# Softmax weights scaled on ScalarE, and another order of the steps in an attention unit

## The chip, the cores and the metric

The kernel runs on one core of one Trainium2 chip. A core has five engines with queues of their own, each of which works strictly in order: TensorE (PE, with PEld for its weight loads), VectorE (DVE), ScalarE (ACT), GpSimd (POOL) and SyncE (SP), which here issues most DMAs. The metric is the device time of one launch in microseconds (us); lower is better.

## The reference

One layer of a bidirectional encoder on x of 256 tokens by 2048 features, in float32. Cut to what matters here:

```python
h = rmsnorm(x, norm1_g)
q, k, v, u = split(h @ w_in)              # 12 query heads, 4 key heads, of 128
scores = q @ k.T * HEAD_DIM**-0.5 + alibi # |t - s| <= 128, else -1e30
m = max(scores.max(-1), sink)
p = exp(scores - m)
p = p / (p.sum(-1) + exp(sink - m))       # the softmax weights
a = rmsnorm(p @ v, attn_out_g)
f = rmsnorm(fourier(u), fourier_out_g)
x = x + concat(a, f) @ w_out
x = x + conv_ffn(rmsnorm(x, norm2_g))     # 2048 -> 2 x 5504 -> 2048
y = rmsnorm(x, normf_g)
```

## The kernel before, in words

**Products in split precision.** A float32 operand of a product is split into a high part (a rounded copy, written by ScalarE) and a low part (the rest, a subtraction on VectorE that reads the high part). A product is three matmuls or fewer: high by high, high by low, low by high. Every weight tile goes through `split` (lines 180 to 189): ScalarE's copy on L185 (128x2048), VectorE's subtraction on L186, then the load of a tile three units later on SP, which needs the raw buffer that was just split.

**Units.** The front of the kernel is a list of units, one weight tile of 1 MB each: slots 4 to 7 make v, slots 8 to 23 make the 16 heads k0, q0, q1, q2, k1, q3, and so on (`QK_ORDER`), slots 24 to 39 are the output projection. After it come the up- and down-projections, which take most of the time. `unit(i, work)` gives TensorE what is listed in `before[i]` and then the unit's own product; it then gives the other engines what is listed in `beside[i]`, splits the weights of unit i+2, and gives them `behind[i]`. All of this is written out by hand (`manual_schedule`): each engine's queue holds its instructions in the order of these calls, and an engine waits at an instruction until its operands are there.

**A head's way through the units.** The loop at L782 lists, for unit i, one step of each head that is d slots behind it:

- d=1: `qk_out` copies half of the product from PSUM on ScalarE (L637, tile `tmp`) and adds on VectorE (L639, `add`); `qk_parts` splits the result into `qT` (ScalarE L234, VectorE L235) or, for a key head, `kT` (L654, L655; a key head has one more VectorE product, L641).
- d=2: `scores` on TensorE (L665); `scores_out` on VectorE (L681 to L686: mask, maximum, `neg`); `exps` on ScalarE (L695, L699), listed behind the unit.
- d=3: `weigh` on VectorE: the sum with the sink's part (L704, `sm`), its reciprocal (L705, `ex`), and two products of 128x256 that scale the softmax weights in place (L708, `sc`). Then `turn`: a VectorE transpose of 32x32 blocks into `tb` (L715), and a DMA of `tb` to DRAM on SP (L720, `turn`).
- d=4: `fetch`: four DMAs on SP that bring the moved blocks back as `td` (L726).
- d=5: `turn_out` splits the moved blocks into `pt` (ScalarE L739, VectorE L740).
- d=6: `values` on TensorE (L768) at the head of the unit; `values_out`: a square and a split on ScalarE (L492, L234 `cat`), the low part on VectorE (L235 `cat`), a running sum on GpSimd (L497).

The last head (q11) is turned on TensorE instead (`turn_last`, L750; `turn_last_out`).

**The four kinds of unit.** Heads come in fours (k, q, q, q), so a unit has one of four sets of steps, by i modulo 4. In these texts they are called A (i = 14, 18, 22), B (15, 19, 23), C (16, 20, 24, and 12 without `turn_out` and `values`) and D (17, 21, and 13 without `values`):

| kind | TensorE, at the head of the unit | VectorE and ScalarE steps before the change, in their order |
|---|---|---|
| A | none | `qk_out` q, `turn_out`, `weigh`, `turn`, `qk_parts` q, split |
| B | `values`, `scores` | `qk_out` q, `turn_out`, `qk_parts` q, `scores_out`, `values_out`, split, `exps` |
| C | `values`, `scores` | `qk_out` q, `turn_out`, `weigh`, `turn`, `qk_parts` q, `scores_out`, `values_out`, split, `exps` |
| D | `values`, `scores` | `weigh`, `turn`, `qk_out` k, `qk_parts` k, `scores_out`, `values_out`, split, `exps` |

At the head of a unit, `values` needs the `pt` of the unit before it, and `scores` the `qT` of the unit before it. "A's steps" below are the VectorE and ScalarE steps listed beside a unit A; the head of unit B on TensorE waits for them.

Of the kernel before, what the change touches and what calls it, by code (L numbers as in the profile page):

```python
# [10 lines left out]
AF = mybir.ActivationFunctionType  # L11
ALU = mybir.AluOpType
# [84 lines left out]
def block_kernel(  # L97
# [18 lines left out]
    nc = tc.nc  # L116
# [297 lines left out]
    before, beside, behind = {}, {}, {}  # L414

    def at(when, i, f, *a):
        when.setdefault(i, []).append((f, a))
# [214 lines left out]
    qk_sb, st = {}, {}  # L632
    sq_a = ph.tile([P, S], F32, tag="sq", name="sq_a")

    def qk_out(kind, h, ps):
        tmp = ph.tile([P, S], F32, tag="tmp", name=f"tmp_{kind}{h}", bufs=2)
        nc.scalar.activation(tmp, ps[:, S : 2 * S], AF.Copy)  # L637
        add = ph.tile([P, S], F32, tag="add", name=f"add_{kind}{h}", bufs=2)
        nc.vector.tensor_tensor(add, ps[:, 0:S], tmp, ALU.add)  # L639
        if kind == "k":  # L640
            nc.vector.tensor_tensor(add, add, r1b, ALU.mult)  # L641
        st["add", kind, h] = add
# [56 lines left out]
        nc.scalar.activation(ex, neg, AF.Exp, bias=vcol(V_SINK + h))  # L699
        st["sc", h] = sc, sm, ex  # L700

    def weigh(h):
        sc, sm, ex = st["sc", h]
        nc.vector.tensor_tensor(sm, sm, ex, ALU.add)  # L704
        nc.vector.reciprocal(ex, sm)  # L705
        for b in range(2):
            s = slice(b * S, (b + 1) * S)
            nc.vector.tensor_scalar(sc[:, s], sc[:, s], ex[:, b : b + 1], None, ALU.mult)  # L708

    def turn(h):  # L710

# [70 lines left out]
    for i in range(N_QK, N_OUT + 8):  # L782
        heads = {i - s: h for (kind, h), s in slot_of.items() if kind == "q"}
        new = [kh for kh, s in slot_of.items() if i - s == 1]
        if i - 9 in range(NG):
            at(before, i, fourier_channels, i - 9)
        valued = [h for d, h in heads.items() if d == (5 if h == NH - 1 else 6)]
        for h in valued:
            at(before, i, values, h, mm if i < N_OUT else dn)
        turned = {d: h for d, h in heads.items() if h < NH - 1}  # L790
        last = {d: h for d, h in heads.items() if h == NH - 1}
        if 4 in last:
            at(before, i, turn_last, last[4])
        if i == 15:
            at(before, i, total, sq_f, "f")
        if 2 in heads:
            at(before, i, scores, heads[2])
        if 4 in turned:
            at(beside, i, fetch, turned[4])

        for kind, h in new:
            if kind == "q":
                at(beside, i, lambda k=kind, h=h: qk_out(k, h, st.pop(("ps", k, h))))
        if 5 in turned:
            at(beside, i, turn_out, turned[5])
        if 4 in last:
            at(beside, i, turn_last_out, last[4])
        if 3 in heads:
            at(beside, i, weigh, heads[3])
        if 3 in turned:  # L810
            at(beside, i, turn, turned[3])
        for kind, h in new:
            if kind == "k":
                at(beside, i, lambda k=kind, h=h: qk_out(k, h, st.pop(("ps", k, h))))
            at(beside, i, qk_parts, kind, h)
        if 2 in heads:
            at(beside, i, scores_out, heads[2])
            at(behind, i, exps, heads[2])
        for h in valued:
            at(beside, i, values_out, h)  # L820
# [60 lines left out]
    for n, (c, kq) in enumerate(OUT_ORDER):  # L881
        i = N_OUT + n
# [391 lines left out]
    i = up_index[n]  # L1274
# [156 lines left out]
```

## Time and profile before

| | |
|---|---|
| time before, median of 3 runs | 910.65 us (909.89 to 910.98) |
| the profiled execution: its time | 908.96 us |
| its span, first to last instruction | 907.2 us |
| mean granted TensorE clock | 0.998 |
| TensorE busy | 893.2 us (98% of the span) |
| VectorE busy | 753.1 us (83%) |
| ScalarE busy | 545.9 us (60%) |
| GpSimd busy | 54.3 us (6%) |

A row of the timeline has the start in us, the duration in us, the engine, the line, the operation, `out<-in` with the shapes, and in brackets the idle time of the engine just before the instruction with what ended it. Rows of instructions that follow each other closely are merged ("x2"), and their duration is then that of the group. An engine starts an instruction before the last one's results are written, so the start of the next row often lies inside the duration of this one: the distance of two starts is called a step here, and the duration counts where another engine waits for the result. In a view of waits a row has the total, the number of waits and the longest, in us. In a view by windows a row has the stretch, its length, and each engine's busy us with its number of instructions; the granted clock, the DMA engines' share and GB/s stand at its end.

### The profile page before, as it was taken

What the parts mean: (1) busy time and instruction counts of PE and PEld (TensorE: products, weight loads), DVE (VectorE), ACT (ScalarE), POOL (GpSimd) and SP (SyncE); (2) the same over time, 40 slices, a digit from 0 to 9 for tenths busy, and PEclk for the clock granted to TensorE, in tenths of its full rate; (3) what the DMA queues carried; (4) which work ended last, traced back from release to release, by engine and by line L of the source; (5) the groups of instructions that cost most, each with busy time, mean ns of one, the idle gap of its engine ahead of it and who ended that gap; (6) DMA issues with size and microseconds to landing.
All of it is one profiled execution on the core that took longest, in us unless ns stands there. A gap on an engine that the chain in (4) does not pass through costs nothing.

```text
span 907.2 us, 12781 instructions
## 1 busy us (share of the span) xinstructions
PE 893.2 (98%) x5020; PEld 804.0 (89%) x5020; DVE 753.1 (83%) x905; ACT 545.9 (60%) x661; POOL 54.3 (6%) x65
## 2 busy tenths in 40 slices
PE   9999999999999999999999999999999999999996
PEld 7899888888899999999999999999999999999885
DVE  7569888777678877889887998978988789998996
ACT  7757576655565656557565566566656566656544
POOL 0001010110000000000000000000000000000004
PEclk9999999999999999999999999999999999999999
DMA  9965666655559687677988779797888987779652
GB/s 360 340 233 174 211 231 197 229 189 191 203 228 290 219 260 235 197 264 215 295 238 276 243 271 278 256 295 232 279 243 244 308 272 255 243 245 286 213 197 92
DMA packets 40827, 220.62 MB, mean 243 GB/s; under 512 B 4512, under 2 KB 10528, under 8 KB 16448
## 3 DMA queue, kind: packets, MB, share of 16 engines
q1 hardware_dynamic: 36512, 190.06, 56.7%
q0 software_dynamic: 4112, 29.49, 17.3%
q8 instruction: 39, 0.64, 0.3%
q10 hardware_dynamic: 144, 0.26, 0.1%
q14 instruction: 20, 0.16, 0.0%
HBM read 214.81 MB, written 4.98 MB: 242 GB/s over the span
## 4 chain that ended last, share of the span: by engine, by line
PE 81%; DVE 8%; DMA 3%; issue 3%; ACT 3%; POOL 1%; SPq 1%; ACTq 0%; POOLq 0%; DVEq 0%
PE ps_val L395 17%; PE ps_gate L395 17%; PE ps_gate L397 8%; PE ps_val L397 8%; PE ps_P L1148 3%; PE ps_P L1150 3%; PE ps_P L1149 3%; PE ps_N L1148 2%; PE ps_N L1150 2%; PE ps_N L1149 2%; DVE parts L186 2%; PE ps_u L289 2%; DMA td<-turn 2%; PE ps_a L380 2%; PE ps_a L378 2%
## 5 line engine op out<-in xcount | busy, mean ns | idle before, releaser
L186 DVE TENSOR_TENSOR parts<-raw,parts 128x2048 fp32r<-128x2048 f32 (+1 forms) x129 | 293.1, 2272 | 43.4 <-ACT parts L185 42.7
L185 ACT ACTIVATE parts<-raw 128x2048 fp32r<-128x2048 f32 (+1 forms) x129 | 245.1, 1901 | 41.7 <-PE ps_a L380 11.9
L395 PE MATMUL ps_val<-hU,parts 128*128 128x512 f32 x688 | 227.7, 382 | 0.0
L395 PE MATMUL ps_gate<-hU,parts 128*128 128x512 f32 x688 | 227.3, 382 | 0.0
L397 PE MATMUL ps_val<-hU,parts 128*128 128x256 f32 x688 | 187.5, 273 | 0.0
L397 PE MATMUL ps_gate<-hU,parts 128*128 128x256 f32 x688 | 186.9, 273 | 0.0
L395 PEld LDWEIGHTS ps_val<-hU,parts 128*128 128x128 f32 x688 | 130.0, 189 | 18.1
L395 PEld LDWEIGHTS ps_gate<-hU,parts 128*128 128x128 f32 x688 | 130.0, 189 | 18.1
L397 PEld LDWEIGHTS ps_val<-hU,parts 128*128 128x128 f32 x688 | 132.0, 192 | 0.8
L397 PEld LDWEIGHTS ps_gate<-hU,parts 128*128 128x128 f32 x688 | 131.8, 192 | 0.9
L926 ACT ACTIVATE ft_g<-ps_gate 128x256 f32<-128x256 f32 x43 | 16.5, 384 | 112.9 <-PE ps_gate L397 110.3
L395 PE MATMUL ps_q<-hT,parts 128*128 128x512 f32 x192 | 62.2, 383 | 0.0
L926 ACT ACTIVATE ft_v<-ps_val 128x256 f32<-128x256 f32 x43 | 16.5, 383 | 73.3 <-PE ps_val L397 73.3
L1148 PE MATMUL ps_P<-parts_P,op_P 128*128 128x512 f32 x144 | 54.7, 380 | 0.0
L1149 PE MATMUL ps_P<-parts_P,op_P 128*128 128x512 f32 x144 | 54.6, 379 | 0.0
L1150 PE MATMUL ps_P<-parts_P,op_P 128*128 128x512 f32 x144 | 54.6, 379 | 0.0
L397 PE MATMUL ps_q<-hT,parts 128*128 128x256 f32 x192 | 50.4, 273 | 0.0
L1034 DVE TENSOR_TENSOR parts_N<-sumw,parts_N 128x2048 fp32r<-128x2048 f32 x18 | 41.2, 2289 | 9.9 <-ACT parts_N L1033 9.9
L1148 PE MATMUL ps_N<-parts_N,op_N 128*128 128x512 f32 x108 | 41.0, 380 | 0.0
L1149 PE MATMUL ps_N<-parts_N,op_N 128*128 128x512 f32 x108 | 40.9, 379 | 0.0
L1150 PE MATMUL ps_N<-parts_N,op_N 128*128 128x512 f32 x108 | 40.9, 379 | 0.0
L395 PEld LDWEIGHTS ps_q<-hT,parts 128*128 128x128 f32 x192 | 36.1, 189 | 4.7
(347 smaller groups left out, 1554.8 us busy)
## 6 DMA issues: line engine op xcount, KB each, us to landing
raw<-in_w_up SPq DMA_DIRECT2D x86, 1024.0 KB, 6.1
raw<-in_w_in SPq DMA_DIRECT2D x20, 1024.0 KB, 5.7
sumw<-in_w_down POOLq DMA_DIRECT2D x18, 1024.0 KB, 8.5
raw<-in_w_out SPq DMA_DIRECT2D x16, 1024.0 KB, 4.8
raw<-in_w_down_late SPq DMA_DIRECT2D x4, 1024.0 KB, 5.7
u_raw<-in_u_in SPq DMA_DIRECT2D x4, 768.0 KB, 10.5
raw<-in_w_down_last SPq DMA_DIRECT2D x4, 768.0 KB, 4.6
turn<-tb SPq DMA_DIRECT2D x11, 256.0 KB, 4.2
```

The lines of the kernel that those rows point to most:

```text
L185: nc.scalar.activation(hi, raw, AF.Copy)
L186: nc.vector.tensor_tensor(lo, raw, f32(hi), ALU.subtract)
L289: nc.tensor.matmul(ps_u[b], block(hk(k), part, b, True), in_turn(w), start=k == 0 and n == 0, stop=k == NK - 1 and n == 2,)
L378: nc.tensor.matmul(ps, ah, wh, start=first and q == q0, stop=False)
L380: nc.tensor.matmul(ps, ah, wl, start=False, stop=last and q == q0 + len(kk) - 1)
L395: nc.tensor.matmul(ps, hi[:, s], in_turn(h), start=k == 0, stop=False)
L397: nc.tensor.matmul(ps[:, 0:S], lo[:, s], in_turn(h)[:, 0:P], start=False, stop=k == NK - 1)
L926: nc.scalar.activation(tmp, ps[:, S : 2 * S], AF.Copy)
L1034: nc.vector.tensor_tensor(lo, src, f32(hi), ALU.subtract)
L1148: nc.tensor.matmul(ps, o[:, 0, p, :], wh, start=first and p == 0, stop=False)
L1149: nc.tensor.matmul(ps, o[:, 1, p, :], wh, start=False, stop=False)
L1150: nc.tensor.matmul(ps, o[:, 0, p, :], wl, start=False, stop=end)
```

## The change

`weigh` becomes two steps. `weights` (sum and reciprocal) stays on VectorE and is listed ahead of `qk_out` of a query head; the new `weigh` scales the softmax weights with two ScalarE copies of 128x256, each with a per-partition scale, in place. `turn_out` goes from its place ahead of `weigh` and `turn` to a place behind `qk_parts`. Nothing else is changed: the DMAs are the same ones, and their order on SP is the same.

```diff
-    def weigh(h):
+    def weights(h):
         sc, sm, ex = st["sc", h]
         nc.vector.tensor_tensor(sm, sm, ex, ALU.add)
         nc.vector.reciprocal(ex, sm)
+
+    def weigh(h):
+        sc, sm, ex = st["sc", h]
         for b in range(2):
             s = slice(b * S, (b + 1) * S)
-            nc.vector.tensor_scalar(sc[:, s], sc[:, s], ex[:, b : b + 1], None, ALU.mult)
+            nc.scalar.activation(sc[:, s], sc[:, s], AF.Copy, scale=ex[:, b : b + 1])
...
+        if 3 in heads:
+            at(beside, i, weights, heads[3])
         for kind, h in new:
             if kind == "q":
                 at(beside, i, lambda k=kind, h=h: qk_out(k, h, st.pop(("ps", k, h))))
-        if 5 in turned:
-            at(beside, i, turn_out, turned[5])
         if 4 in last:
             at(beside, i, turn_last_out, last[4])
         if 3 in heads:
...
             at(beside, i, qk_parts, kind, h)
+        if 5 in turned:
+            at(beside, i, turn_out, turned[5])
         if 2 in heads:
             at(beside, i, scores_out, heads[2])
             at(behind, i, exps, heads[2])
```

## The prediction

> **What bounds the kernel now.** I read the page first, then TensorE's waits, then the attention stage by windows, then each engine's timeline there.
>
> ```profile
> span 907.2 us, 12781 instructions
> PE 893.2 (98%) x5020; PEld 804.0 (89%) x5020; DVE 753.1 (83%) x905; ACT 545.9 (60%) x661; POOL 54.3 (6%) x65
> ```
>
> TensorE is busy for 98% of the span, so the change can only pay where TensorE waits. The view of its weight loads' waits names the places:
>
> ```profile
> PEld ps_o L768 <- DVE pt L740: 3.5, 4, 1.1
> PEld ps_s L665 <- DVE qT L235: 3.1, 4, 1.1
> PEld ps_o L768 <- ACT pt L739: 0.7, 2, 0.4
> ```
>
> That is 7.3 us, all in the attention units, at four places: the heads of the units B and the unit of the last turn. It is the ceiling of any gain here. The view by windows shows one round of four units, A to D, as VectorE goes through them:
>
> ```profile
> 118.38:123.50 5.12, 3.44 (x23) 2.94 (x22) 5.02 (x11) 2.50 (x3) 0.00 (x0) 1.00 0.73 238
> 123.50:130.52 7.02, 7.02 (x47) 6.53 (x46) 5.15 (x12) 5.26 (x12) 0.93 (x1) 1.00 0.76 241
> 130.52:137.82 7.30, 7.30 (x52) 6.85 (x51) 7.05 (x18) 5.19 (x11) 0.74 (x1) 1.00 0.48 180
> 137.82:145.96 8.14, 8.02 (x50) 7.20 (x49) 6.86 (x17) 5.47 (x11) 1.00 (x1) 1.00 0.61 193
> ```
>
> A's steps begin with `add_q`; in the first and the third round that is here (timeline):
>
> ```profile
> 91.14 0.41 DVE L639 TENSOR_TENSOR add_q<-ps_q,tmp_q 128x256 f32<-128x256 f32 x1
> 145.96 0.42 DVE L639 TENSOR_TENSOR add_q<-ps_q,tmp_q 128x256 f32<-128x256 f32 x1
> ```
>
> A round takes 27.58 us (5.12 + 7.02 + 7.30 + 8.14); VectorE is busy for 24.08 of it (third engine column), ScalarE for 18.42. TensorE's rows:
>
> ```profile
> 119.45 0.38 PE L768 MATMUL ps_o<-pt,v_hi 128*128 128x256 f32 x1 [0.74 <-DVE pt L740]
> 121.43 0.71 PE L665 MATMUL ps_s<-kT,qT 128*128 128x256 f32 x4 [0.93 <-DVE qT L235]
> 121.98 0.38 PE L395 MATMUL ps_q<-hT,parts 128*128 128x512 f32 x1
> 127.22 0.39 PE L768 MATMUL ps_o<-pt,v_hi 128*128 128x256 f32 x2
> 128.56 0.60 PE L395 MATMUL ps_k<-hT,parts 128*128 128x512 f32 x2
> 173.11 0.38 PE L380 MATMUL ps_a<-parts,cat 128*128 128x512 f32 x1
> 175.00 0.30 PE L750 MATMUL ps_t<-ident,sc 128*128 128x128 f32 x1
> ```
>
> An unhindered unit head takes 1.34 us (127.22 to 128.56, 12 matmuls, 0.11 each), its product 5.24 (121.98 to 127.22). Three heads and four products make 25.0, some 2.6 less than the round. So in these units **the round of VectorE with its waits is the bound**, and TensorE takes up the difference at the head of B. What counts is the length of that round, and how late in A's steps `pt` and `qT` are.
>
> **The change, part by part.** A's steps now, on VectorE and on ScalarE:
>
> ```profile
> 118.38 0.42 DVE L639 TENSOR_TENSOR add_q<-ps_q,tmp_q 128x256 f32<-128x256 f32 x1
> 118.71 0.68 DVE L740 TENSOR_TENSOR pt<-td,pt 128x512 fp32r<-128x512 f32 x1
> 119.31 0.16 DVE L704 TENSOR_TENSOR sm<-sm,ex 128x2 f32<-128x2 f32 x1
> 119.50 0.17 DVE L705 RECIPROCAL ex<-sm 128x2 f32<-128x2 f32 x1
> 119.71 0.62 DVE L708 TENSOR_SCALAR sc<-sc,ex 128x256 f32<-128x256 f32 x2
> 120.36 0.71 DVE L715 STREAM_TRANSPOSE tb<-sc 128x512 f32<-128x512 f32 x1
> 120.99 0.38 DVE L235 SCALAR_TENSOR_TENSOR qT<-add_q,qT 128x256 fp32r<-128x256 f32 x1
> 121.30 2.28 DVE L186 TENSOR_TENSOR parts<-raw,parts 128x2048 fp32r<-128x2048 f32 x1
> ```
>
> ```profile
> 117.64 0.64 ACT L739 ACTIVATE pt<-td 128x512 fp32r<-128x512 f32 x1
> 118.83 0.44 ACT L234 ACTIVATE qT<-add_q 128x256 fp32r<-128x256 f32 x1 [0.56 <-DVE add_q L639]
> 119.18 1.89 ACT L185 ACTIVATE parts<-raw 128x2048 fp32r<-128x2048 f32 x1
> 124.81 0.63 ACT L739 ACTIVATE pt<-td 128x512 fp32r<-128x512 f32 x1 [3.47 <-DMA td<-turn]
> 125.34 0.49 ACT L234 ACTIVATE qT<-add_q 128x256 fp32r<-128x256 f32 x1
> 125.73 0.37 ACT L492 ACTIVATE sq<-ps_o 128x256 f32<-128x256 f32 x1
> 126.00 0.47 ACT L234 ACTIVATE cat<-ps_o,vec 128x256 fp32r<-128x256 f32 x1
> 126.36 1.92 ACT L185 ACTIVATE parts<-raw 128x2048 fp32r<-128x2048 f32 x1
> ```
>
> In B, VectorE waits for that `pt` of 124.81:
>
> ```profile
> 125.47 0.69 DVE L740 TENSOR_TENSOR pt<-td,pt 128x512 fp32r<-128x512 f32 x1 [1.56 <-ACT pt L739]
> ```
>
> See that ScalarE runs ahead: it splits A's `pt` at 117.64, before VectorE begins A at 118.38, and has finished the weight split (121.07) when VectorE comes to it (121.30).
>
> *Removed:* per query head two VectorE products, 0.65 us by their step (119.71 to 120.36). *Added:* two ScalarE copies with a per-partition scale. The trace has no such 128x256 row; the nearest are the same operation at 512 columns and a 256-column one without the scale operand:
>
> ```profile
> 896.99 0.70 ACT L1201 ACTIVATE xs<-xs,rstd 128x512 f32<-128x512 f32 x1
> 894.93 1.32 ACT L1201 ACTIVATE xs<-xs,rstd 128x512 f32<-128x512 f32 x2
> 898.94 0.42 ACT L1160 ACTIVATE junkc<-xs 128x256 f32<-128x256 f32 x1
> L695 ACT ACTIVATE sc<-sc,neg,rq_pos 128x256 f32<-128x256 f32 x24 | 14.2, 596 | 7.6 <-DVE neg L686 7.6
> ```
>
> 256 columns fewer cost 0.21 (0.63 for `pt` of 512 columns, 0.42 here), so one copy takes 0.70 - 0.21 = 0.49, and its step 0.62 - 0.21 = 0.41. I take 0.50 and 0.41. Bounds for the pair: 0.27 + 0.37 = 0.64, at the unscaled 256-column `sq` (0.37; step 125.73 to 126.00), and 2 x 0.60 = 1.20, at the exponentials with two operands and without overlap. My 0.91 lies nearest to the row of the same operation. The Trainium skill (ScalarE: Activation LUTs, What ACT_TABLE_LOAD costs) gives 186 ns + 0.833 ns per element, 93 ns more per pointer operand, and back-to-back overlap of 93 ns; an estimate from that page is 492 ns and a step of 399, a pair of 0.89, which would put the sum below 0.2 us lower; the exponentials' 596 ns agree with its 585.
>
> *The new wait.* The copies need the reciprocal, so ScalarE can't start them before VectorE has begun the unit, and behind them wait `qT`, `pt` and the weight split, for which VectorE then waits. From VectorE's begin of a unit (t = 0): sum, reciprocal ready at 0.36; handing over takes 0.04 (118.80 to 118.83 is such a case); copies from 0.40 and 0.81, **done at 1.31**; transpose from 1.34 (the addition of `add_q` fits in the gap). Then, by the steps above:
>
> - A: ScalarE `qT` 1.22, `pt` 1.61, weight split 2.14 to 4.06. VectorE `qT` 1.97, `pt` 2.35 to 3.03, then idle until 4.09, split for 2.20 (121.30 to 123.50): 6.29, was 5.12.
> - B: no scaling here. The wait for `td` (1.56 on VectorE) is hidden: `td` lands 6.4 after A's begin, ScalarE comes to it at 6.29 + 0.81. `qT` 0.46, `pt` 0.81, `sq` 1.34, `cat` 1.61, weight split 1.97 to 3.89, VectorE's split to 6.12, was 7.02.
> - C: `qT` 1.22, `pt` 1.61, `sq` 2.14, `cat` 2.41, weight split 2.77 to 4.69, VectorE's split to 6.92, was 7.30.
> - D: no `turn_out`. The transpose comes at 1.34 where it came 1.05 after the sum (119.31 to 120.36), and all that follows is 0.29 later: 8.43, was 8.14.
>
> The round is 6.29 + 6.12 + 6.92 + 8.43 = **27.76, was 27.58**: the wait costs what the lighter VectorE saves. A longer `td` landing would cost only above the 0.7 us of cover in B. The turn DMA leaves in A 0.6 us earlier, and SP's order is as before; that earns nothing, as `td` no longer comes last.
>
> *The sum.* First A: unit 12 is a C with `add_q` ahead, so its transpose moves from 0.33 + 1.05 = 1.38 to 1.34, -0.04; unit 13 is a D, +0.29. A begins at 91.39. Two rounds later it is 91.39 + 55.52 = 146.91, before 145.96: +0.95. Then the head of B: `values` waited for a `pt` that came early and `scores` for `qT`, and TensorE was free 3.60 after A's begin (121.98). Now `pt` is last, at 3.03; plus 0.06 until TensorE takes it (119.39 to 119.45), plus the head less its first matmul, 1.23: 4.32, +0.72. TensorE is 1.67 late from there on. At the last place it had arrived at 173.33 (173.11 + 0.22), and its transposes stood at 175.00, 1.00 later than the 0.67 of six matmuls allows; that stall was due to `pt` and is swallowed: `pt` is ready as before, since C of the third round ends at 146.91 + 19.33 = 166.24. 1.67 - 1.00 leaves **+0.67 us**; behind that TensorE has no such wait. The profiled execution goes from 908.96 (span 907.2, 1.76 around it) to 909.63; the median stands 1.69 above that execution, so 910.65 + 0.67 = 911.3.
>
> **The rivals.** *Slower:* the scaling pair on ScalarE is longer than I take it. Its end enters nine times (units 12 and 13, six in two rounds, the last `pt`). At 1.20 instead of 0.91 that is 9 x 0.29 = 2.6 more: 913.9. It counts as slower from a pair of 1.04, 0.13 above mine (0.67 + 9 x 0.13 = 1.8). For it: ScalarE's chain has no slack in A, B and C. Against: the 512-column row is the same operation. The Trainium skill (same page, Rules for kernel authors) gives multiplications to VectorE rather than ScalarE, which speaks for this side; the rows agree in direction, 0.65 against 0.91.
>
> *Faster:* VectorE is really relieved, ScalarE's wait is covered, and the round falls to TensorE's 25.0. Then up to all 7.3 us go: 903.4. For it: VectorE's 24.08 busy less three pairs is about 22, and ScalarE has 9 idle us per round. Against: both queues are in order and hand work to and fro within a unit. The pair at its lower bound, 0.64, gives 9 x 0.27 = 2.4 less: 908.9, just at the edge.
>
> **How the numbers follow.** About 0.2%, 1.8 us, is what a measurement of this kernel can tell from no change. Forecast (the waits take back the gain, within 0.2%): 0.50. Slower by the longer chain: 0.34. Faster: 0.16, of which the stalls gone altogether have a third. The range reaches from the lower bound of the pair, a little beyond it for a part of the faster case, 908.5, to its upper bound, 913.9.
>
> **What would show it.** In the changed profile A's steps should take about 6.3, with VectorE idle before L186 in A on ScalarE's L185; B's wait on `td` should be gone; D about 8.4; TensorE's waits at the heads of B should be on `pt` alone, about 3 us each, and none be left at 174. I am wrong if rounds are under 27 (then the pair or the hand-over is shorter), or if ScalarE's split is done before VectorE wants it in A and C.

## The result and the profile after

The changed kernel takes 912.88 us (median of 8 runs, 910.97 to 913.23), the kernel before 910.50 beside it (8 runs, 908.47 to 912.06): a ratio of 1.0023, 95% interval 1.0012 to 1.0034. In a second measurement on one chip with other versions (label `e5_after_again` below) it is 1.0016 (1.0007 to 1.0025). So it is slower by 1.5 to 2.1 us, at the edge of the 0.2% that the forecast called no change; 911.3 was predicted.

The profiled execution took 910.97 us with a span of 908.9, the lowest of its eight. Its granted clock, 0.996, is the highest of them; six of the eight have 0.992, so this profile shows the less usual kind. The page's first lines:

```profile
span 908.9 us, 12795 instructions
PE 894.5 (98%) x5020; PEld 805.9 (89%) x5020; DVE 744.6 (82%) x881; ACT 555.8 (61%) x685; POOL 54.7 (6%) x65
```

VectorE is busy for 8.5 us less (753.1 before), ScalarE for 9.9 more (545.9), and the span is 1.7 longer. TensorE's weight loads wait elsewhere than before:

```profile
PEld ps_o L771 <- ACT pt L742: 5.3, 3, 2.8
PEld ps_o L771 <- DVE pt L743: 2.0, 4, 0.6
```

The waits for `qT` are gone, and those for `pt` are longer, up to 2.8 us at a time where 1.1 was the longest. The first round by windows, from A's begin, with units A, B, C, D in this order:

```profile
92.13:98.36 6.23, 3.55 (x17) 3.36 (x18) 4.46 (x8) 3.81 (x6) 0.00 (x0) 0.77 0.81 253
98.36:104.53 6.17, 6.17 (x40) 5.68 (x40) 5.30 (x13) 5.21 (x11) 0.72 (x1) 0.95 0.74 212
104.53:111.49 6.96, 6.96 (x50) 6.54 (x49) 6.01 (x15) 5.62 (x12) 1.05 (x1) 1.00 0.56 192
111.49:119.93 8.44, 8.44 (x53) 7.75 (x53) 6.25 (x15) 6.08 (x13) 0.98 (x1) 1.00 0.58 187
```

The units take 6.23, 6.17, 6.96 and 8.44 us; 6.29, 6.12, 6.92 and 8.43 were predicted. What was not predicted stands in the third column from the right: TensorE's granted clock is 0.77 in A and 0.95 in B. A's steps in the third round, on VectorE:

```profile
148.11 0.15 DVE L704 TENSOR_TENSOR sm<-sm,ex 128x2 f32<-128x2 f32 x1
148.30 0.17 DVE L705 RECIPROCAL ex<-sm 128x2 f32<-128x2 f32 x1
148.38 0.41 DVE L639 TENSOR_TENSOR add_q<-ps_q,tmp_q 128x256 f32<-128x256 f32 x1
149.50 0.71 DVE L718 STREAM_TRANSPOSE tb<-sc 128x512 f32<-128x512 f32 x1 [0.71 <-ACT sc L711]
150.13 0.38 DVE L235 SCALAR_TENSOR_TENSOR qT<-add_q,qT 128x256 fp32r<-128x256 f32 x1
150.44 0.68 DVE L743 TENSOR_TENSOR pt<-td,pt 128x512 fp32r<-128x512 f32 x1
152.14 2.29 DVE L186 TENSOR_TENSOR parts<-raw,parts 128x2048 fp32r<-128x2048 f32 x1 [1.02 <-ACT parts L185]
```

and on ScalarE:

```profile
148.56 0.91 ACT L711 ACTIVATE sc<-sc,ex 128x256 f32<-128x256 f32 x2 [1.08 <-DVE ex L705]
149.37 0.41 ACT L234 ACTIVATE qT<-add_q 128x256 fp32r<-128x256 f32 x1
149.69 0.61 ACT L742 ACTIVATE pt<-td 128x512 fp32r<-128x512 f32 x1
150.21 1.90 ACT L185 ACTIVATE parts<-raw 128x2048 fp32r<-128x2048 f32 x1
```

See the chain: ScalarE idles 1.08 us until the reciprocal is there, and VectorE then idles 0.71 for the scaling and 1.02 for the weight split. The pair of copies takes 0.91, as taken in the prediction.

What the long wait does to TensorE, at the head of the first B (timeline, then the granted clock by windows):

```profile
91.58 0.27 PE L397 MATMUL ps_q<-hT,parts 128*128 128x256 f32 x1
94.37 0.38 PE L771 MATMUL ps_o<-pt,v_hi 128*128 128x256 f32 x1 [2.52 <-ACT pt L742]
95.19 0.38 PE L771 MATMUL ps_o<-pt,v_hi 128*128 128x256 f32 x1 [0.44 <-DVE pt L743]
95.40 0.31 PE L771 MATMUL ps_o<-pt,v_lo 128*128 128x256 f32 x1
95.94 0.42 PE L771 MATMUL ps_o<-pt,v_lo 128*128 128x256 f32 x1
98.28 0.63 PE L395 MATMUL ps_q<-hT,parts 128*128 128x512 f32 x1
98.71 0.38 PE L397 MATMUL ps_q<-hT,parts 128*128 128x256 f32 x1
```

```profile
91.00:95.40 4.40, 1.44 (x8) 0.93 (x7) 3.39 (x8) 3.24 (x7) 0.92 (x1) 1.00 0.68 227
95.40:98.80 3.40, 3.40 (x17) 3.31 (x17) 2.63 (x2) 0.99 (x2) 0.00 (x0) 0.52 0.60 169
```

After a wait of 2.52 and one of 0.44 us the clock is granted at about half (0.52) for 3.4 us: a matmul of 512 columns that takes 0.38 elsewhere takes 0.63. Such a stretch loses 3.4 x 0.5 = 1.7 us of TensorE's time, and 1.7 / 909 = 0.0019 of the mean clock of the execution.

### The profile page after: what moved, and what is told of

Its sections match the earlier page's. It is cut to its first block, busy times and chain, and to the rows that moved or that the text cites. A ratio compares the mean times of both kernels' runs of the same rounds, so it can differ in the third digit from the quotient of the medians.

```text
span 908.9 us, 12795 instructions
## 1 busy us (share of the span) xinstructions
PE 894.5 (98%) x5020; PEld 805.9 (89%) x5020; DVE 744.6 (82%) x881; ACT 555.8 (61%) x685; POOL 54.7 (6%) x65
## 4 chain that ended last, share of the span: by engine, by line
PE 84%; DVE 7%; ACT 6%; issue 2%; POOL 1%; ACTq 0%; POOLq 0%; DVEq 0%
PE ps_val L395 17%; PE ps_gate L395 17%; PE ps_gate L397 8%; PE ps_val L397 8%; DVE parts L186 3%; PE ps_P L1153 3%; PE ps_P L1155 3%; PE ps_P L1154 3%; ACT parts L185 3%; PE ps_N L1153 2%; PE ps_N L1155 2%; PE ps_N L1154 2%; PE ps_u L289 2%; PE ps_a L380 2%; PE ps_a L379 2%
```

## The experiments

**Theory 1** (the prediction's): the round of VectorE's and ScalarE's steps, chained through the reciprocal, sets the pace, and the end of the scaling pair enters nine times. **Theory 2** (formed on the profile above): part of the loss is the clock, halved behind each long wait. **Rivals**: VectorE is really relieved, and the new order costs; ScalarE's work is hidden; the clock is a side effect. Four kernels at a time ran on one chip (the last two by themselves); each ratio is to the kernel before on that chip. All times are medians.

### One part alone

The copies on ScalarE in the order of before:

```diff
-            nc.vector.tensor_scalar(sc[:, s], sc[:, s], ex[:, b : b + 1], None, ALU.mult)
+            nc.scalar.activation(sc[:, s], sc[:, s], AF.Copy, scale=ex[:, b : b + 1])
```

> Scaling on ScalarE, all steps in the order of before. Theory 1 (ScalarE's chain behind the reciprocal sets the round): the reciprocal comes 0.93 us later in a unit, after the addition and the low part of pt, so the copies end 2.24 after the unit's begin; A 6.7, B 7.0 with its wait on td, C 7.3, D 8.4, a round of 29.4 against 27.6 before and 27.8 after. Two rounds and the two units ahead: 4 us and more over before, about 914.5 to 916. Rival (the work taken off VectorE is a gain, the new order is what costs): as fast as before or faster, at most 910.5.

Measured: 914.53 us, ratio 1.0046 (1.0033 to 1.0060), by theory 1. Its two rounds by windows:

```profile
92.01:121.13 29.12, 26.50 (x169) 24.01 (x169) 22.02 (x48) 20.80 (x42) 2.66 (x3) 1.00 0.62 199
121.13:150.29 29.16, 27.39 (x165) 24.93 (x165) 22.00 (x47) 20.86 (x42) 2.76 (x3) 0.94 0.60 198
```

VectorE is busy for 22.0 us instead of 24.1 in a round, and the rounds are 1.9 and 1.6 us longer than before (27.24 and 27.58): taking work off an engine gains nothing where the engine then waits for it.

The new order with the scaling on VectorE, against the changed kernel:

```diff
-            nc.scalar.activation(sc[:, s], sc[:, s], AF.Copy, scale=ex[:, b : b + 1])
+            nc.vector.tensor_scalar(sc[:, s], sc[:, s], ex[:, b : b + 1], None, ALU.mult)
```

> The new order, scaling on VectorE as before. Theory 1: ScalarE has qT and pt done early again; A 5.8, B 6.1 with the wait on td hidden, C 6.7, D 8.1, a round of 26.8; the head of B starts 4.3 after A's begin instead of 3.6, as pt is late. In all about 1.8 us less than before: 908.7. The clock stays at full if the waits at the heads of B stay under 2 us. Rival (the new order is what costs): 911.5 or more.

Measured: 908.82 us, ratio 0.9974 (0.9965 to 0.9983). So the order is the gain and the copies on ScalarE are the loss; the rival that the order costs is out. The rounds:

```profile
119.93:147.10 27.17, 27.17 (x179) 25.26 (x178) 24.08 (x54) 18.38 (x36) 2.74 (x3) 1.00 0.66 213
91.17:119.93 28.76, 26.32 (x151) 24.23 (x151) 24.14 (x55) 18.41 (x36) 2.51 (x3) 0.88 0.61 202
```

The second round (first row) is near the 26.8 expected, the first is not: its granted clock is 0.88. Behind waits of 1.62 and 0.82 us at the head of B the clock was at half for 6.8 us (94.0 to 100.8); in C, ScalarE then waited 2.53 for TensorE's product, and VectorE for ScalarE's copy of it:

```profile
104.99 0.42 DVE L639 TENSOR_TENSOR add_q<-ps_q,tmp_q 128x256 f32<-128x256 f32 x1 [1.70 <-ACT tmp_q L637]
```

The expectation that waits under 2 us leave the clock alone was wrong.

### The length of the scaling

One copy on ScalarE, one product on VectorE, side by side:

```diff
-            nc.scalar.activation(sc[:, s], sc[:, s], AF.Copy, scale=ex[:, b : b + 1])
+            if b == 0:
+                nc.scalar.activation(sc[:, s], sc[:, s], AF.Copy, scale=ex[:, b : b + 1])
+            else:
+                nc.vector.tensor_scalar(sc[:, s], sc[:, s], ex[:, b : b + 1], None, ALU.mult)
```

> As after, but one of the two scalings on VectorE and one on ScalarE, side by side. Theory 1: the transpose can start 1.08 after the unit's begin instead of 1.34, ScalarE's chain is 0.41 shorter; A 5.9, C 6.5, D 8.2, a round of 26.7. About 2.7 us under the sum predicted for after, 908.6. Rival (ScalarE's copies are hidden, the loss is the clock alone or the order alone): within 1 us of after.

Measured: 906.37 us, ratio 0.9953 (0.9939 to 0.9967), faster than both kernels and 2.2 us faster than expected. The rounds are as expected, 26.57 and 26.83 for 26.7:

```profile
90.49:117.06 26.57, 24.74 (x152) 22.70 (x151) 22.86 (x51) 19.54 (x39) 2.77 (x3) 0.94 0.66 218
117.06:143.89 26.83, 26.83 (x177) 25.00 (x176) 22.90 (x50) 19.63 (x39) 3.04 (x3) 1.00 0.65 216
```

Its profiled span is 904.5, 2.7 under that of before's profiled execution, where the expected sum has 2.0. The medians lie 4.8 apart: before's median on this chip (911.13) is 2.2 above its profiled execution (908.96), and why is not known.

The same work in four copies:

```diff
-            s = slice(b * S, (b + 1) * S)
-            nc.scalar.activation(sc[:, s], sc[:, s], AF.Copy, scale=ex[:, b : b + 1])
+            for o in (0, P):
+                part = sc[:, b * S + o : b * S + o + P]
+                nc.scalar.activation(part, part, AF.Copy, scale=ex[:, b : b + 1])
```

> The changed kernel with each scaling copy cut into two of 128 columns, the same work in four ScalarE instructions. Theory 1 (the end of the scaling enters nine times): by the slope of 0.21 us per 256 columns a copy's step is 0.30, the four end 1.69 after the unit's begin instead of 1.31, 9 x 0.38 = 3.4 us more than the changed kernel: about 916.3. Rival (ScalarE has 9 idle us in a round and hides them): as the changed kernel, 912.9.

Measured: 915.54 us, ratio 1.0047 (1.0035 to 1.0060); the changed kernel beside it 912.12. In the profiles the four copies take 1.28 us, 0.37 more than the pair. Nine times that is 3.3, and 3.4 was measured (within the intervals, 1 us either way); the clock, 0.990 to 0.995 here, may have a share in it. Its rounds, 28.9 by theory 1:

```profile
92.41:121.49 29.08, 26.23 (x153) 24.20 (x154) 22.05 (x49) 21.65 (x48) 2.72 (x3) 0.88 0.64 200
121.49:150.51 29.02, 27.88 (x180) 25.47 (x178) 21.92 (x47) 21.82 (x48) 2.99 (x3) 1.00 0.62 199
```

### The place in A

As the version with halves, but in A `turn_out` and `qk_parts` come ahead of the scaling, which is all on VectorE there:

```diff
+        early = i in (14, 18, 22)
+        if early:
+            for kind, h in new:
+                at(beside, i, lambda k=kind, h=h: qk_out(k, h, st.pop(("ps", k, h))))
+            at(beside, i, turn_out, turned[5])
+            for kind, h in new:
+                at(beside, i, qk_parts, kind, h)
         if 3 in heads:
             at(beside, i, weights, heads[3])
...
-            at(beside, i, weigh, heads[3])
+            at(beside, i, weigh, heads[3], early)
```

> One scaling on ScalarE and one on VectorE in C and D, the new order in B, C and D; in A, pt and qT come ahead of the scaling, which is all on VectorE there. Theory 1 (what counts is the round and how late pt and qT are in A): A 5.3, B 6.1, C 6.5, D 8.2, a round of 26.1, and TensorE free 2.4 after A's begin instead of 3.6 before: 4.4 us less than before, and the wait of 1.0 at the last place goes too: 905.1 to 905.7. Rival (only the round counts): as the version with halves everywhere, 906.4 or more.

Measured: 906.29 us, ratio 0.9952 (0.9938 to 0.9965): as the halves, not the 1 us better that was expected. The rounds:

```profile
91.13:116.98 25.85, 25.29 (x166) 23.41 (x165) 23.20 (x52) 18.99 (x38) 2.78 (x3) 1.00 0.68 224
116.98:143.66 26.68, 26.29 (x172) 24.14 (x170) 23.15 (x52) 19.22 (x38) 3.01 (x3) 1.00 0.67 217
```

The clock is full, and the first round is 25.85. In the second, a wait of the kernel before came back: A takes only 5.15 us there (116.98 to 122.13; 5.12 before), so ScalarE comes to `td` in B before the fetch that SP issued beside A, from 117.49 on, has landed:

```profile
123.71 0.63 ACT L745 ACTIVATE pt<-td 128x512 fp32r<-128x512 f32 x1 [0.61 <-DMA td<-turn]
```

So neither theory's number came out; the rival's time did, but by another wait.

### The clock

The changed kernel again, 11 executions:

> The changed kernel as it is, beside the next three on one chip. Theory 2 (TensorE's clock is halved behind long waits): granted clock 0.992 in most executions, about 912.9, and executions with a higher clock are faster, about 1 us for each 0.002. Rival: time and clock are unrelated.

Measured: 912.12 us, ratio 1.0016 (1.0007 to 1.0025). Of its 19 executions in both measurements, 13 have a clock of 0.992 and a mean of 912.75, 3 have 0.994 and 911.73, 3 have 0.996 and 910.71: the clocks are what three, two and one slow stretch of 0.0019 each take from 0.998, and the means are 1 us apart. Time and clock are related, as theory 2 has it. Where three stretches lie is not shown: both profiled executions have 0.996, with their one stretch behind the first wait.

The changed kernel with work for TensorE in the wait (`FILL` 10, then 11):

```diff
+    def fill(i):
+        ps = bank(dn, f"ps_fill{i}")
+        for _ in range(FILL):
+            nc.tensor.matmul(ps, one, ones_512, start=True, stop=True)
...
+        if i in (15, 19, 23):
+            at(before, i, fill, i)
```

> As after, with ten extra matmuls (128x512, bf16, 0.22 us each, 2.2 us in all) of constants into an unused bank at the head of each of the three units B, where TensorE otherwise waits for pt; their result is not used. Theory 2 (the part of the loss beyond the longer chain is TensorE's clock, halved for 3.4 us behind a wait of 2.5 us): the granted clock goes from 0.992 to 0.998, the time from 912.9 to about 911.2. Rival (the clock is a side effect, the loss is in the chain): unchanged at 912.9 or, if the extra matmuls delay TensorE, higher.

> The changed kernel with eleven extra matmuls of constants (2.4 us) at the head of each unit B, results unused. Theory 2: granted clock 0.998, 1 to 2 us less than the changed kernel beside it. Rival (the clock's loss is swallowed by the next wait anyway): no difference.

Measured: 911.54 us with ten, ratio 1.0011 (1.0002 to 1.0019), clock 0.997 to 0.999 in all executions; 910.85 with eleven, ratio 0.9999 (0.9990 to 1.0007), where the changed kernel beside it stood at 1.0016. In the profile with eleven the same stretch runs at full clock:

```profile
90.76 2.58 PE L788 MATMUL ps_fill<-const-bfloat16-1.0 128*128 128x512 bf16 x11
93.44 0.38 PE L772 MATMUL ps_o<-pt,v_hi 128*128 128x256 f32 x1
```

```profile
95.40:98.80 3.40, 3.40 (x24) 3.19 (x24) 2.79 (x3) 0.97 (x3) 0.00 (x0) 1.00 0.54 127
```

With eleven, matmuls that compute nothing take 1.3 us off the changed kernel beside them, so the clock is a cause and not a side effect. With ten, no changed kernel ran beside them, and 1.0011 alone is not clear of its 1.0016. The profile with ten also has a cost of another kind: in the third B, at full clock, ScalarE waits 0.99 for `td`, which lands 8.2 us after A's begin, beyond the cover that the prediction gave it. The next two runs ask which of the stretches counts, with ten extra matmuls at the third B alone (`if i == 23`) or at the first two (`if i in (15, 19)`):

> The changed kernel with ten extra matmuls of constants at the head of the third unit B alone, results unused. Theory 2, refined: the slow stretches behind the first and second long wait are swallowed by the next wait, since VectorE's round goes on meanwhile, and only that behind the third reaches the end: granted clock about 0.994 to 0.996, time as with all three filled, ratio to before about 1.000 to 1.001. Rival (each slow stretch costs alike): a third of the gain, ratio 1.0015.

> The changed kernel with ten extra matmuls at the heads of the first and second unit B, none at the third, results unused. Theory 2, refined: granted clock up to about 0.996, but the time as the changed kernel, ratio 1.0016 to 1.0023, since the third wait is as long as before. Rival (each slow stretch costs alike): two thirds of the gain, ratio 1.0005.

Measured: the third alone 910.86 us, ratio 1.0002 (0.9993 to 1.0011), clock 0.993 to 0.996, as the refined theory has it. The first two alone: 910.55 us, ratio 0.9996 (0.9987 to 1.0005), where the refined theory wanted 1.0016 or more and the rival 1.0005. The changed kernel did not run on this chip, so that both fillings help rests on its 1.0016 and 1.0023 elsewhere.

What a stretch costs can be read from the profiles. With the first two filled, a slow stretch follows the third wait (1.89 and 0.44 us):

```profile
149.81 0.38 PE L772 MATMUL ps_o<-pt,v_hi 128*128 128x256 f32 x1 [1.89 <-ACT pt L743]
152.32 0.63 PE L396 MATMUL ps_q<-hT,parts 128*128 128x512 f32 x1
177.75 0.60 PE L754 MATMUL ps_t<-ident,sc 128*128 128x128 f32 x4
```

In the changed kernel's profile none follows a third wait of nearly the same length (1.93 and 0.44):

```profile
150.36 0.38 PE L771 MATMUL ps_o<-pt,v_hi 128*128 128x256 f32 x1 [1.93 <-ACT pt L742]
152.50 0.38 PE L395 MATMUL ps_q<-hT,parts 128*128 128x512 f32 x1
176.84 0.60 PE L753 MATMUL ps_t<-ident,sc 128*128 128x128 f32 x4
```

From the third A's begin (147.56 and 148.11) to the transposes of the last place it is 30.19 us with the stretch and 28.73 without, so here a stretch costs 1.46 us. Behind the first wait it costs nothing: the first round takes 27.80 us with it (the changed kernel) and without it (the first two filled). TensorE comes to the second B 2.47 us after A's begin instead of 0.91, and waits less there, 0.17 and 0.35. So the refined theory holds in the traces. Its time for the first two filled did not come out, and by the clock the third stretch was rare in these executions: the three with a clock of 0.996, of which the profiled one has that stretch, have a mean of 911.46, the eight above have 910.37. Why it came so seldom is open.

## Why the prediction was right, and what it lacked

- **The bound and the chain**: right. The round of VectorE with its waits sets the pace; A 6.23, B 6.17, C 6.96, D 8.44 measured for 6.29, 6.12, 6.92, 8.43. The copies took 500 ns each, 0.91 a pair, as taken. The version with the copies alone, the one with the order alone, the halves and the four copies moved their rounds to what the chain foretold, within 0.4 us except in the first round with the order alone, where the slowed clock reached VectorE.
- **The second round** was 28.18 instead of 27.76: its A took 6.63, since the copies started 0.3 late, behind `add_q`, where the others started behind the reciprocal:

```profile
L711 ACT ACTIVATE sc<-sc,ex 128x256 f32<-128x256 f32 x24 | 10.9, 500 | 14.2 <-DVE ex L705 12.8 <-DVE add_q L639 1.4
```

  It is one of twelve pairs (the 1.4 at the end of the row), the same one in both profiles of the changed kernel; its cause is open.
- **Head of B**: right in what TensorE waits for, `pt` alone, and in when it is free in the third round, 4.4 after A's begin (4.32 predicted). Waits of about 3 us were forecast at three places; in the profile they are 2.96, 0.52 and 2.37, the second short since TensorE came late. The wait at the last place is gone, as predicted.
- **The wait on `td` in B**: gone in the changed kernel's profile, as predicted; it came back where A was short again (`e7_early_a`) and in the profile with ten extra matmuls.
- **The sum**, +0.67, is the step that fell short. The transposes of the last place stand at 176.84 after and 175.00 before; unit 12 began 0.66 later in this execution (75.86 against 75.20) before the first changed step had run, so between these two profiles the units themselves cost 1.2. Of the 0.5 beyond the sum, 0.4 is the second round above.
- **The clock** is a term that the sum did not have. The prediction forecast waits of about 3 us at three places and counted them at their length only. In the profile the one slow stretch costs nothing, but most executions have a clock of 0.992, and with eleven extra matmuls the changed kernel is level with the kernel before (0.9999; with ten 1.0011). So the medians put most of the loss down to the clock, while the profiles of before and after put 1.2 us of it down to the units. Before's profiled execution lies 1.5 us under its median (910.50), for a reason that is not known; how the measured 1.5 to 2.1 us divide between the two is therefore open. The Trainium skill (TensorE: Matmul & The Clock Gate, The HAM clock gate) states that the clock falls to half after an idle window of about 3.4 us, free-running, and rises again after about 3.4 us of sustained work; the trace agrees with the half and with the 3.4 us of slow running, but here waits of 2.5 and 0.4 were enough. By that figure a wait of about 3 us is too short to halve the clock; the measurement decides otherwise.
- **Luck**: that the time came within 1.6 us of 911.3 is in part chance. The sum gives the changed kernel before's 1.69 us between the profiled execution and the median; it has 1.91, but beside a clock of 0.996 in the profiled execution and 0.992 in most others.
- **The rivals**: the slower one decides at a pair of 1.04; the pair was 0.91, so the price of the copies did not send the time to that side. The faster one, VectorE relieved, is refuted by the copies alone, 1.0046, and was half right in its kind: with half of the scaling on each engine the round does fall, to 26.7.

## What to carry to other kernels

Moving an operation to an idler engine pays only if what stands behind it in that engine's queue isn't waited for: write out both queues for one unit, with each hand-over, before believing the busy shares. An operation that two engines can do may be best split between them, so that neither waits for the whole. And a wait on TensorE is not paid at its length alone: look at the granted clock in the windows right behind it.

## What the runs showed of the hardware

- The granted clock fell to about half for 3.4 us behind waits well under that: behind 2.52 and 0.44 us in the changed kernel, and behind 1.35 and 0.47 in the version with halves, where this row is the first of its slow stretch:

```profile
93.55 0.64 PE L774 MATMUL ps_o<-pt,v_hi 128*128 128x256 f32 x2
```

- It does not fall each time: in the changed kernel's profile the waits of 1.93 and 0.44 at the third B left the clock at 1.00; with the first two filled, waits of 1.89 and 0.44 at the same place halved it. Executions of one kernel differ, 0.992 to 0.996.
- A slow stretch costs nothing where the next wait swallows it (the first round, 27.80 us with and without) and 1.46 us where no such wait follows, against the 1.7 us of TensorE's time that it loses.
- The kernel before spreads over 909.1 to 912.9 us on one chip; the clock doesn't explain that (there, executions with 0.993 have a mean of 911.4 and those with 0.998 of 910.7; on the chip of the last two versions, 0.994 has 910.1 and 0.998 has 911.1), and its cause is open.
